# RWKV-7 scan: the prepared product X a taken apart into two products inside each step

## The chip, the cores and the metric

The kernel runs on one core of a Trainium2 chip. The metric is the device time of one execution in microseconds; the median of several executions is quoted. Four engines compute and run side by side, each through its own queue in order: PE (matrix products), DVE (vector), ACT (scalar) and POOL (GpSimd); SP issues the DMAs. They wait for each other by semaphores.

## The reference, cut to what matters

An encoder with four layers. Layers 0 and 3 mix by latent attention, layer 1 by RWKV-7, layer 2 by an RG-LRU; after each mixer stands a convolutional gated feed-forward block. The change touches the recurrence of layer 1 alone: 16 heads of 64, 528 tokens, forwards and backwards.

```python
def _wkv7_scan(r, w, a, b, k, v, reverse):
    def step(S, inp):
        r_t, w_t, a_t, b_t, k_t, v_t = inp
        sa = jnp.einsum('bhvk,bhk->bhv', S, a_t)
        S = S * w_t[:, :, None, :] + sa[..., None] * b_t[:, :, None, :] + v_t[..., None] * k_t[:, :, None, :]
        return S, jnp.einsum('bhvk,bhk->bhv', S, r_t)
    ...
    _, y = lax.scan(step, S0, xs, reverse=reverse)
```

## The kernel before

**The recurrence in windows.** `rwkv_scan` cuts the 528 tokens into nine windows (eight of 64 tokens and one of 16) and works on a pair of heads at a time, one head on partitions 0 to 63 and the other on 64 to 127. Eight pairs and two directions make 16 *chains*, numbered i = 0 to 15. Inside a window the recurrence is solved with a triangular inverse X (tile `xt`); from window to window only the 64x64 state S is handed on.

**What a chain needs.** For each chain four streams of instructions prepare tiles:
- `stage_a`: decays, keys and queries of all windows. `xr[:, 0]` holds the rows a, `xr[:, 1]` the rows r, `bk` the rows b and k; the products of `bk` with `xr`, masked, are `am` (`am[:, 1, w, 0:64]` is A_ak of window w, `am[:, 0, w, 0:64]` is A_ab). `stage_a` also starts the streams below.
- `inverses`: inverts the 16x16 diagonal blocks on POOL, by way of two trips through DRAM (`sc`, `sd`). Its last step on chip is an ACT copy `dt<-dt` that waits for POOL.
- `stage_b`: joins the blocks to the full X in `xt`, with products into the bank `rb` and DVE between them.
- `a_tokens` (turns a into `at`), `bk_tokens` (turns b and k into `tb`), `ak_v` (A_ak v of all windows at once, into `r1`). They use `per_window`: 18 products of 64x64, then two ACT copies out of PSUM, one of 512 columns and one of 64. The end of `stage_b` makes `xa` = X a in the same way.

**A step of a chain** (`chain`, from L1644). For window w the bank `pu` gets X r1, issued one step ahead, and then `xa` times S; DVE copies it to `u`. The bank `ps` gets the products of `tb` with v and with u; DVE turns it into the next state S (tile `s1`), with the decayed old state `sp` from POOL. Products of `am`, `xr` and v, u, S go to `yp`, the output, and are waited for only at the chain's end. So from one S to the next the path runs: PE (`ch<-s,xa`), DVE (`u<-ch`), PE (`ch<-u,tb`), DVE (`s<-ch,pc,sp`). The banks of `pu` and `ps` come from a pool of two, called `ch`. A chain can begin when the chain before it has been issued.

**What sets the order.** `Streams.run` is a list scheduler that runs while the kernel is built. It holds a cost for each operation and a latency for each pair of engines, and writes out one fixed order for each engine; the streams' priorities come from `AHEAD`, and a later chain's preparation is woven between the steps of the chain that runs. Where its plan leaves PE idle for long and the products planned shortly before are few, `fill` puts in products that nobody reads (`idle<-hid_w`, 128x256), called fillers below. On the chip each engine takes its instructions in the written order, whatever the real times are.

One product of 64x64 in the code appears in the trace as two matrix instructions.

Of the kernel before, what the change touches and what calls it, by code (L numbers as in the profile page):

```python
# [143 lines left out]
class Streams:  # L144
# [13 lines left out]
    def take(self, kind):  # L158
        return ("take", kind)

    def give(self, t):
        return ("give", t)

    def wait(self, *names):
        return ("wait", names)

    def spawn(self, name, gen, prio=0.0):
        return ("spawn", name, gen, prio)
# [157 lines left out]
class Kern:  # L326
# [999 lines left out]
    def rwkv_scan(self, es, hid, rkv, yall):  # L1326
        nc, a, tc = self.nc, self.a, self.tc
        sch = Streams(nc, SLACK)
        pe, ve, ac, po, dq = sch.pe, sch.dve, sch.act, sch.pool, sch.dma
# [5 lines left out]
        def tl(shape, name, bufs=1, dt=F32):  # L1335
            return sch.named(cp.tile(shape, dt, name=name, tag=name, bufs=bufs), name, bufs)
# [25 lines left out]
        N9 = NW + 1  # L1362
# [15 lines left out]
        E = [slice(64 * e, 64 * e + 64) for e in range(2)]  # L1378
# [3 lines left out]
        def prio(kind, i):  # L1382
            return AHEAD[kind] - i
# [43 lines left out]
        def turned(src, out):  # L1427

            yield from per_window(lambda w, e: src(w)[E[e]], lambda w, e: self.ident[E[e], E[e]], lambda ps, ws: ac.copy(out[:, ws], ps))
# [40 lines left out]
        def stage_a(i, hp, d, P, U):  # L1470
# [42 lines left out]
            else:  # L1513
                yield ve.scalar_tensor_tensor(out=xr[:, 0, 0:T - 1], in0=kk[:, 0:T - 1], scalar=-2.0, in1=ep[:, 1:T], op0=ALU.mult, op1=ALU.mult)
                yield ve.tensor_scalar(out=xr[:, 0, 63:T:64], in0=kk[:, 63:T:64], scalar1=-2.0, scalar2=None, op0=ALU.mult)
                yield ve.tensor_scalar(out=xr[:, 0, T - 1:T], in0=kk[:, T - 1:T], scalar1=-2.0, scalar2=None, op0=ALU.mult)
            yield spawn(f"at{i}", a_tokens(i, xr, U), prio("at", i))
            yield ve.tensor_tensor(out=xr[:, 1, 0:T], in0=P["r"], in1=ep, op=ALU.mult)
            yield ve.tensor_copy(pc[:, 0:NW], ep[:, (0 if d else 63):SEQ:64])
            yield ve.tensor_copy(pc[:, NW:NW + 1], ep[:, SEQ:SEQ + 1])  # L1520
# [21 lines left out]
                    yield give(pa)  # L1542
            yield spawn(f"inv{i}", inverses(i, d, U), prio("inv", i))
            yield spawn(f"tb{i}", bk_tokens(bk, U), prio("tb", i))
            yield spawn(f"r1{i}", ak_v(i, hp, P, U), prio("r1", i))
            if d:
                yield po.tensor_tensor(out=P["kds"], in0=P["kds"], in1=kd, op=ALU.add)

        def a_tokens(i, xr, U):
            if i >= 2:  # L1550
                yield wait(f"b{i - 2}")
            U["at"] = tl([128, N9, 64], "at", 2)
            yield from turned(lambda w: xr[:, 0, w * 64:w * 64 + 64], U["at"])

        def bk_tokens(bk, U):
            tb = U["tb"] = tl([128, 2, N9, 64], "tb", DEEP)
            for j in range(2):
                yield from turned(lambda w: bk[:, j, w], tb[:, j])

        def ak_v(i, hp, P, U):  # L1560
            yield wait(f"values{hp}", *([f"c{i - 3}"] if i >= 3 else []))
            r1 = U["r1"] = tl([128, N9, 64], "r1", 3)
            yield from per_window(lambda w, e: U["am"][E[e], 1, w, 0:64], lambda w, e: P["vt"][E[e], w], lambda ps, ws: ac.copy(r1[:, ws], ps))

        def inverses(i, d, U):

# [34 lines left out]


        def stage_b(i, hp, d, P, U):
            yield wait(f"inv{i}", f"at{i}", f"r1{i}", *([f"b{i - 1}"] if i else []))
            am, dc = U["am"], U["dc"]
            dd = [tl([128, NW, 4, 16], f"dd{j}") for j in range(2)]
            for j in (1, 0):
                yield ve.tensor_tensor(out=dd[j], in0=dc[:, j].unsqueeze(2).to_broadcast([128, NW, 4, 16]),
                                       in1=blk.unsqueeze(1).to_broadcast([128, NW, 4, 16]), op=ALU.mult)
            dtr, dn = (t.rearrange("p w q t -> p w (q t)") for t in dd)  # L1610
            nn = tl([128, NW, 64], "nn")

            def product(lhsT, rhs):
                ps = yield take("rb")
                for w in range(NW):
                    for e in range(2):
                        r = rhs(w, e)
                        yield pe.matmul(win(ps)[E[e], w, 0:r.shape[-1]], lhsT=lhsT(w, e), rhs=r, start=True, stop=True)
                return ps

            ps = yield from product(lambda w, e: am[E[e], 0, w, 0:64], lambda w, e: dn[E[e], w])
            yield ve.tensor_tensor(out=nn, in0=win(ps), in1=offb.unsqueeze(1).to_broadcast([128, NW, 64]), op=ALU.mult)
            yield give(ps)
            if i >= 2:
                yield wait(f"c{i - 2}")
            xt = U["xt"] = xts[i % 2]
            ps = yield from product(lambda w, e: nn[E[e], w], lambda w, e: dtr[E[e], w])
            yield ve.tensor_tensor(out=xt[:, 0:NW], in0=win(ps), in1=dtr, op=ALU.add)
            yield give(ps)

            b0 = 32 * d
            for lo, hi, c0, c1 in ((b0, b0 + 32, 32 - b0, 64 - b0), (b0, 16 + 48 * d, 48 * (1 - d), 64 - 48 * d)):
                n = c1 - c0
                ps = yield from product(lambda w, e: nn[E[e], w], lambda w, e: xt[E[e], w, c0:c1])
                for e in range(2):
                    r = slice(64 * e + lo, 64 * e + hi)
                    yield ve.tensor_tensor(out=xt[r, 0:NW, c0:c1], in0=win(ps)[r, :, 0:n], in1=dtr[r, :, c0:c1], op=ALU.add)
                yield give(ps)

            xa = U["xa"] = tl([128, N9, 64], "xa", 2)  # L1640
            yield from per_window(lambda w, e: U["at"][E[e], w], lambda w, e: xt[E[e], w], lambda ps, ws: ac.copy(xa[:, ws], ps))


        def chain(i, hp, d, P, U):  # L1644
            yield wait(f"b{i}", f"r1{i}", f"tb{i}", *([f"c{i - 1}"] if i else []))
            am, xr, v, pc, y, tb = U["am"], U["xr"], P["vt"], U["pc"], yall[:, hp], U["tb"]
            u = tl([128, N9, 64], "u")
            yt = yield take("yp")
            yp = win(yt)
            order = list(range(N9))[::-1 if d else 1]  # L1650

            def both(o, lhsT, rhs, start, stop):
                for e in range(2):
                    yield pe.matmul(o[E[e]], lhsT=lhsT[E[e]], rhs=rhs[E[e]], start=start, stop=stop)

            S = None
            pu = yield take("ch")
            yield from both(pu[:, 0:64], U["xt"][:, order[0]], U["r1"][:, order[0]], True, True)
            for w, after in zip(order, order[1:] + [None]):
                n = 16 if w == NW else 64  # L1660
                rw = xr[:, 1, w * 64:w * 64 + n]

                if S is not None:
                    yield from both(pu[:, 0:64], U["xa"][:, w], S, False, True)
                if after is not None:
                    p1 = pc[:, w:w + 1]
                    if S is not None:
                        sp = tl([128, 64], "sp", 2)
                        yield po.tensor_tensor(out=sp, in0=S, in1=p1.to_broadcast([128, 64]), op=ALU.mult)
                    ps = yield take("ch")  # L1670
                    yield from both(ps[:, 0:64], tb[:, 1, w], v[:, w], True, False)
                yield ve.tensor_copy(u[:, w], pu[:, 0:64])
                yield give(pu)
                if after is not None:
                    yield from both(ps[:, 0:64], tb[:, 0, w], u[:, w], False, True)
                    pu = yield take("ch")
                    yield from both(pu[:, 0:64], U["xt"][:, after], U["r1"][:, after], True, False)
                    s1 = tl([128, 64], "s1", 3)
                    if S is None:
                        yield ve.tensor_scalar(out=s1, in0=ps[:, 0:64], scalar1=p1, scalar2=None, op0=ALU.mult)  # L1680
                    else:
                        yield ve.scalar_tensor_tensor(out=s1, in0=ps[:, 0:64], scalar=p1, in1=sp, op0=ALU.mult, op1=ALU.add)
                    yield give(ps)
                yo = (yield take("ps")) if w == NW else yp[:, w]
                yield from both(yo[:, 0:n], v[:, w], am[:, 1, w, 64:64 + n], True, False)
                if S is not None:
                    yield from both(yo[:, 0:n], S, rw, False, False)
                yield from both(yo[:, 0:n], u[:, w], am[:, 0, w, 64:64 + n], False, True)
                if w == NW:
                    if d:  # L1690
                        yield ve.tensor_tensor(out=y[:, SEQ:], in0=y[:, SEQ:], in1=yo[:, 0:16], op=ALU.add)
                    else:
                        yield ac.copy(y[:, SEQ:], yo[:, 0:16])
                    yield give(yo)
                S = s1
            if d:
                yield ve.tensor_tensor(out=w64(y), in0=w64(y), in1=yp, op=ALU.add)
            else:
                yield ac.copy(w64(y), yp)
            yield give(yt)  # L1700
# [204 lines left out]
```

## Time and profile before

| | |
|---|---|
| median of 3 runs | 3550.47 us (3542.97 to 3557.28) |
| profiled execution | 3547.82 us, span 3546.0 us |
| PE busy | 3229.4 us (91% of the span) |
| DVE busy | 2799.9 us (79%) |
| ACT busy | 1610.5 us (45%) |
| POOL busy | 1003.2 us (28%) |
| stage of the 16 chains | from 1099.7 to 1572.8 us |

A busy share is the union of the instructions' durations; products are pipelined and overlap, so a busy PE may still have room. Times inside the span are counted from its start. "Granted clock" is the share of full speed that TensorE's throttle let through.

### The profile page before, as it was taken

To read this page: it belongs to the slowest core of one execution; us is meant where nothing else is said; L and a number is where in the kernel's file an instruction comes from. 1 tells how busy PE (TensorE), PEld (TensorE's weight loads), DVE (VectorE), ACT (ScalarE), POOL (GpSimd) and SP (SyncE) were. 2 spreads that over 40 slices of the span, in tenths; PEclk is the share of its full clock that TensorE was granted. 3 is DMA by queue.
4 is the path that set the end of the run, shared out by engine and by line. 5 is a ranking of instruction groups with operands and counts; after the bars stand their busy time and mean duration, and the time that the engine had idled before them with its cause. 6 is when DMAs were issued, how large, how long until landed. Compare 5 with 4: busy or idle time off the path is not lost.

```text
span 3546.0 us, 77810 instructions
## 1 busy us (share of the span) xinstructions
PE 3229.4 (91%) x31961; PEld 3099.3 (87%) x31961; DVE 2799.9 (79%) x5158; ACT 1610.5 (45%) x3035; POOL 1003.2 (28%) x1438
## 2 busy tenths in 40 slices
PE   5999889997988888878899988989999899989998
PEld 5899889996977877868899988979999799979998
DVE  5877799979436767657999779789997787789997
ACT  4765444333333333324333468643334666543433
POOL 0000253323006455434533200045431000045341
PEclk9999999998989999989999989999999999999999
DMA  2011213322422112122233222213332011212332
GB/s 82 22 40 38 75 63 103 103 84 86 136 77 48 35 38 45 25 53 88 82 105 97 87 72 72 79 54 100 98 94 81 20 37 34 66 43 93 103 92 71
DMA packets 155557, 250.06 MB, mean 71 GB/s; under 512 B 78496, under 2 KB 85824, under 8 KB 154944
## 3 DMA queue, kind: packets, MB, share of 16 engines
q1 hardware_dynamic: 155200, 245.08, 22.7%
q8 instruction: 251, 4.11, 0.5%
q14 instruction: 106, 0.87, 0.1%
HBM read 227.93 MB, written 17.10 MB: 69 GB/s over the span
## 4 chain that ended last, share of the span: by engine, by line
PE 59%; DVE 22%; ACT 8%; issue 5%; POOL 3%; DMA 2%; SPq 0%; DVEq 0%; ACTq 0%; POOLq 0%
PE bank L424 13%; PE bank L422 13%; PE bank L423 13%; PE pj L218 8%; PE ps L218 3%; DVE wlo L577 3%; PE s L218 3%; PE ch L218 1%; ACT wv L218 1%; PE rb L218 1%; DVE cv L699 1%; DVE pst L218 1%; DVE gp L640 1%; DVE cv L705 1%; DVE wlo L411 1%
## 5 line engine op out<-in xcount | busy, mean ns | idle before, releaser
L422 PE MATMUL bank<-xhi,whi 128*128 128x264 f32 x2144 | 608.3, 289 | 38.6 <-ACT xhi L416 28.9
L423 PE MATMUL bank<-xlo,whi 128*128 128x264 f32 x2144 | 618.3, 290 | 23.7 <-DVE xlo L564 12.5
L424 PE MATMUL bank<-xhi,wlo 128*128 128x264 f32 x2144 | 613.0, 289 | 23.4 <-DVE wlo L577 21.6
L422 PEld LDWEIGHTS bank<-xhi,whi 128*128 128x128 f32 x2144 | 406.3, 192 | 41.2 <-ACT xhi L416 28.8
L423 PEld LDWEIGHTS bank<-xlo,whi 128*128 128x128 f32 x2144 | 410.4, 191 | 33.1 <-DVE xlo L564 17.8
L424 PEld LDWEIGHTS bank<-xhi,wlo 128*128 128x128 f32 x2144 | 409.4, 192 | 29.7 <-DVE wlo L577 27.2
L424 PE MATMUL bank<-phi,wlo 128*128 128x264 f32 x1408 | 401.2, 285 | 2.1 <-DVE wlo L411 2.1
L422 PE MATMUL bank<-phi,whi 128*128 128x264 f32 x1408 | 400.5, 284 | 0.0
L423 PE MATMUL bank<-plo,whi 128*128 128x264 f32 x1408 | 400.3, 284 | 0.0
L576 ACT CAST whi<-wraw 128x1024 fp32r<-128x1024 f32 (+1 forms) x240 | 217.3, 907 | 263.9 <-PE bank L423 164.4
L577 DVE TENSOR_TENSOR wlo<-wraw,whi 128x1024 fp32r<-128x1024 f32 (+1 forms) x240 | 321.3, 1340 | 10.5 <-ACT whi L576 10.0
L411 DVE TENSOR_TENSOR wlo<-wraw,whi 128x1024 fp32r<-128x1024 f32 (+1 forms) x218 | 243.7, 1118 | 105.1 <-ACT whi L410 102.3
L410 ACT CAST whi<-wraw 128x1024 fp32r<-128x1024 f32 (+1 forms) x218 | 205.6, 946 | 198.8 <-PE bank L423 140.6
L424 PE MATMUL bank<-thi,wlo 128*128 128x264 f32 x960 | 276.2, 288 | 21.3 <-DVE wlo L577 21.3
L423 PE MATMUL bank<-tlo,whi 128*128 128x264 f32 x960 | 274.7, 286 | 0.0
L422 PE MATMUL bank<-thi,whi 128*128 128x264 f32 x960 | 273.9, 286 | 0.0
L424 PEld LDWEIGHTS bank<-phi,wlo 128*128 128x128 f32 x1408 | 264.8, 188 | 2.8 <-DVE wlo L411 2.8
L422 PEld LDWEIGHTS bank<-phi,whi 128*128 128x128 f32 x1408 | 265.1, 188 | 0.0
L423 PEld LDWEIGHTS bank<-plo,whi 128*128 128x128 f32 x1408 | 264.7, 188 | 0.0
L591 POOL TENSOR_TENSOR wraw<-wraw,wsum 128x512 f32<-128x512 f32 x80 | 113.4, 1418 | 384.7 <-DVE wlo L577 313.1
L424 PEld LDWEIGHTS bank<-thi,wlo 128*128 128x128 f32 x960 | 182.6, 190 | 23.8 <-DVE wlo L577 23.8
L422 PEld LDWEIGHTS bank<-thi,whi 128*128 128x128 f32 x960 | 182.9, 191 | 0.0
(402 smaller groups left out, 9841.1 us busy)
## 6 DMA issues: line engine op xcount, KB each, us to landing
wraw<-in_ffn_in_dram SPq DMA_DIRECT2D x176, 512.0 KB
wraw<-in_ffn_out_dram SPq DMA_DIRECT2D x96, 384.0 KB
wraw<-in_mla_o_dram SPq DMA_DIRECT2D x48, 256.0 KB
wraw<-in_rw_rkv_dram SPq DMA_DIRECT2D x24, 512.0 KB
wraw<-in_lru_in_dram SPq DMA_DIRECT2D x20, 512.0 KB
wraw<-in_mla_q_dram SPq DMA_DIRECT2D x16, 512.0 KB
wraw<-in_ffn_out_dram SPq DMA_DIRECT2D x16, 512.0 KB
rkv<-ro SPq DMA_DIRECT2D x24, 264.0 KB
```

What stands on the lines that cost most here:

```text
L218: op.fn(*op.args, **op.kw)
L410: nc.scalar.copy(hi[:, :cols], raw[:, :cols])
L411: nc.vector.tensor_tensor(out=lo[:, :cols], in0=raw[:, :cols], in1=hi[:, :cols].bitcast(F32), op=ALU.subtract)
L422: nc.tensor.matmul(out, lhsT=w[0][ws], rhs=x[0][xs], start=start, stop=False)
L423: nc.tensor.matmul(out, lhsT=w[0][ws], rhs=x[1][xs], start=False, stop=False)
L424: nc.tensor.matmul(out, lhsT=w[1][ws], rhs=x[0][xs], start=False, stop=stop)
L576: nc.scalar.copy(hi[:, cut], x[:, cut])
L577: nc.vector.tensor_tensor(out=lo[:, cut], in0=x[:, cut], in1=hi[:, cut].bitcast(F32), op=ALU.subtract)
L591: e.tensor_tensor(out=a1[:, 1], in0=a1[:, 1], in1=s[:, 1], op=ALU.subtract)
L640: add = lambda out, x: nc.vector.tensor_tensor(out=out, in0=x, in1=ps, op=ALU.add)
L699: nc.vector.scalar_tensor_tensor(out=c, in0=gp[:, q:q + T], scalar=self.p(f"fc_w{l}{q}", f), in1=c, op0=ALU.mult, op1=ALU.add)
L705: nc.vector.tensor_tensor(out=c, in0=c, in1=dst[j][:, 1:T + 1], op=ALU.mult)
```

## The change

The step computes W = A_ak v + a S first, copies it out of PSUM, and then multiplies by X. The stream `a_tokens` with its tile `at`, the stream `ak_v` with `r1`, and the product `xa` at the end of `stage_b` are gone; `stage_b` and `chain` no longer wait for them, and `chain` waits for `values` (the tile `vt` of v) instead. A step takes three banks one after the other from the same pool of two: `pw`, `ps`, `pu`.

```diff
@@ stage_a
-            yield spawn(f"at{i}", a_tokens(i, xr, U), prio("at", i))
...
-            yield spawn(f"r1{i}", ak_v(i, hp, P, U), prio("r1", i))
...
-        def a_tokens(i, xr, U):
-            if i >= 2:
-                yield wait(f"b{i - 2}")
-            U["at"] = tl([128, N9, 64], "at", 2)
-            yield from turned(lambda w: xr[:, 0, w * 64:w * 64 + 64], U["at"])
...
-        def ak_v(i, hp, P, U):
-            yield wait(f"values{hp}", *([f"c{i - 3}"] if i >= 3 else []))
-            r1 = U["r1"] = tl([128, N9, 64], "r1", 3)
-            yield from per_window(lambda w, e: U["am"][E[e], 1, w, 0:64], lambda w, e: P["vt"][E[e], w], lambda ps, ws: ac.copy(r1[:, ws], ps))
@@ stage_b
-            yield wait(f"inv{i}", f"at{i}", f"r1{i}", *([f"b{i - 1}"] if i else []))
+            yield wait(f"inv{i}", *([f"b{i - 1}"] if i else []))
...
-            xa = U["xa"] = tl([128, N9, 64], "xa", 2)
-            yield from per_window(lambda w, e: U["at"][E[e], w], lambda w, e: xt[E[e], w], lambda ps, ws: ac.copy(xa[:, ws], ps))
@@ chain
-            yield wait(f"b{i}", f"r1{i}", f"tb{i}", *([f"c{i - 1}"] if i else []))
+            yield wait(f"b{i}", f"values{hp}", f"tb{i}", *([f"c{i - 1}"] if i else []))
...
-            pu = yield take("ch")
-            yield from both(pu[:, 0:64], U["xt"][:, order[0]], U["r1"][:, order[0]], True, True)
+            pw = yield take("ch")
+            yield from both(pw[:, 0:64], am[:, 1, order[0], 0:64], v[:, order[0]], True, True)
...
-                    yield from both(pu[:, 0:64], U["xa"][:, w], S, False, True)
+                    yield from both(pw[:, 0:64], xr[:, 0, w * 64:w * 64 + 64], S, False, True)
+                x = tl([128, 64], "x", 2)
+                yield ac.copy(x, pw[:, 0:64])
+                yield give(pw)
...
+                pu = yield take("ch")
+                yield from both(pu[:, 0:64], U["xt"][:, w], x, True, True)
                 yield ve.tensor_copy(u[:, w], pu[:, 0:64])
                 yield give(pu)
...
-                    pu = yield take("ch")
-                    yield from both(pu[:, 0:64], U["xt"][:, after], U["r1"][:, after], True, False)
+                    pw = yield take("ch")
+                    yield from both(pw[:, 0:64], am[:, 1, after, 0:64], v[:, after], True, False)
```

Since the scheduler writes the order anew, rows move on every engine. On PE, in the last chain, two steps before the change stand like this (`ch<-s,xa` is X a times S, `ch<-r,xt` is X r1 of the next step, `ch<-u,tb` the product that makes the next state; "x2" is the two heads):

```order
L218 MATMUL ch_20280<-s_20283,xa 64x64 x2
L218 MATMUL ch_20295<-vt_11278,tb 64x64 x2
L218 MATMUL ch_20295<-u,tb 64x64 x2
L218 MATMUL ch_20301<-r_19508,xt_11280 64x64 x2
L218 MATMUL yp_20184<-am,vt_11278 64x64 x2
L218 MATMUL yp_20184<-xr,s_20283 64x64 x2
L218 MATMUL yp_20184<-am,u 64x64 x2
L218 MATMUL ch_20301<-s_20304,xa 64x64 x2
```

and after the change, at the same place (`ch<-s,xr` is a S, `ch<-x,xt` is X W, `ch<-vt,am` is A_ak v of the next step):

```order
L218 MATMUL ch_19993<-s_19996,xr 64x64 x2
L218 MATMUL ch_20010<-vt_11278,tb 64x64 x2
L218 MATMUL ch_20013<-x,xt_11280 64x64 x2
L1739 MATMUL idle<-hid_w_9613 128x256 x4
L218 MATMUL ch_20010<-u,tb 64x64 x2
L218 MATMUL ch_20023<-vt_11278,am 64x64 x2
L218 MATMUL yp_19861<-am,vt_11278 64x64 x2
L218 MATMUL yp_19861<-xr,s_19996 64x64 x2
L218 MATMUL yp_19861<-am,u 64x64 x2
L218 MATMUL ch_20023<-s_20026,xr 64x64 x2
```

A third product on the path, `ch<-x,xt`, now stands between the product with S and the one with u, and in this step four fillers behind it.

In the middle of the stage, where later chains are prepared, a step before the change has on PE (`rb` is `stage_b` of a later chain, `ps<-ident,bk` its `bk_tokens`):

```order
L218 MATMUL ch_16266<-s_16269,xa 64x64 x2
L218 MATMUL ch_16285<-vt_11278,tb 64x64 x2
L218 MATMUL rb_16230<-dd_16177,am 64x64 x7
L218 MATMUL ch_16285<-u,tb 64x64 x2
L218 MATMUL ch_16298<-r_15073,xt_11280 64x64 x2
L218 MATMUL ps_16146<-vt_11277,am 64x64 x9
```

and after it, at a similar place:

```order
L218 MATMUL ch_16586<-s_16591,xr 64x64 x2
L218 MATMUL rb_16520<-dd_16384,nn 64x64 x4
L218 MATMUL ch_16613<-vt_11277,tb 64x64 x2
L218 MATMUL rb_16520<-dd_16384,nn 64x64
L218 MATMUL ch_16616<-x,xt_11279 64x64 x2
L218 MATMUL ps_16563<-hid_a_9653,w2hi 128x264
L218 MATMUL ps_16563<-hid_a_9653,w2lo 128x264
L218 MATMUL ps_16555<-rs_y,rwcst 128x132
...
L218 MATMUL ch_16613<-u,tb 64x64 x2
```

The preparation is now dealt out over three gaps of a step in place of two; the nine `ps<-vt,am` (the batched A_ak v) have no counterpart.

On ACT, behind the copy `dt<-dt` that waits for POOL, stands before the change, at two places in the middle of the stage:

```order
L218 COPY dt<-dt 66x256
L218 COPY at<-ps_15442 128x512
L218 COPY at<-ps_15479 128x64
...
L218 COPY dt<-dt 66x256
L218 ACTIVATE c<-ps_16060,half_b 128x264
L218 COPY tb<-ps_16144 128x512
```

and after it, at two places there:

```order
L218 COPY dt<-dt 66x256
L218 COPY x<-ch_15213 128x64
L218 ACTIVATE c<-ps_15267,half_b 128x264
L218 COPY x<-ch_15259 128x64
...
L218 COPY dt<-dt 66x256
L218 COPY x<-ch_15766 128x64
L218 COPY x<-ch_15818 128x64
```

The copy `x` of the running chain stands directly behind `dt<-dt` at ten of its sixteen places; before, no instruction of a running step was on ACT.

## Rows read from the trace of the kernel before

**Rows 1.** The page: the span, and each engine's busy time.
```profile
span 3546.0 us, 77810 instructions
PE 3229.4 (91%) x31961; PEld 3099.3 (87%) x31961; DVE 2799.9 (79%) x5158; ACT 1610.5 (45%) x3035; POOL 1003.2 (28%) x1438
```
**Rows 2.** Windows: ahead of the chains, the stage of the chains, behind it.
```profile
core 0: us, PE busy (x) PEld busy (x) DVE busy (x) ACT busy (x) POOL busy (x), PEclk, DMA share, GB/s
1070.00:1100.00 30.00, 22.98 (x479) 19.52 (x478) 16.80 (x39) 11.76 (x28) 22.62 (x59) 0.89 0.30 65
1099.70:1572.80 473.10, 417.98 (x9542) 379.70 (x9540) 308.90 (x840) 142.84 (x341) 239.12 (x600) 0.95 0.17 35
1580.00:1600.00 20.00, 13.30 (x74) 12.48 (x73) 10.23 (x17) 8.94 (x15) 2.17 (x3) 0.62 0.55 187
```
**Rows 3.** Tile u: duration ns min/median/max, first and last start us.
```profile
L218 PE MATMUL ch<-u,tb x512: 216/218/367, 1101.8 to 1571.4; 64*64 64x64 f32 x171
L218 DVE COPY u<-ch x144: 199/224/226, 1100.7 to 1572.4; 128x64 f32<-128x64 f32 x144
```
**Rows 4.** Timeline, one step of the last chain: start us, duration us.
```profile
1563.02 0.28 DVE L218 SCALAR_TENSOR_TENSOR s<-ch,pc,sp 128x64 f32<-128x64 f32 x1 [0.51 <-PE ch L218]
...
1563.36 0.33 PE L218 MATMUL ch<-s,xa 64*64 64x64 f32 x4
...
1563.74 0.22 DVE L218 COPY u<-ch 128x64 f32<-128x64 f32 x1 [0.43 <-PE ch L218]
1564.02 0.33 PE L218 MATMUL ch<-u,tb 64*64 64x64 f32 x4 [0.21 <-DVE u L218]
...
1564.47 0.28 DVE L218 SCALAR_TENSOR_TENSOR s<-ch,pc,sp 128x64 f32<-128x64 f32 x1 [0.50 <-PE ch L218]
...
1564.81 0.33 PE L218 MATMUL ch<-s,xa 64*64 64x64 f32 x4
```
**Rows 5.** Timeline of PE: runs of equal products, with the row behind.
```profile
1355.32 0.37 PE L218 MATMUL ps<-hid_a,w2hi 128*128 128x264 f32 x1
1355.53 0.28 PE L218 MATMUL ps<-hid_a,w2lo 128*128 128x264 f32 x1
1355.74 1.09 PE L218 MATMUL ps<-xr,bk 64*64 64x128 f32 x16
1356.66 0.28 PE L218 MATMUL yp<-am,vt 64*64 64x64 f32 x4
...
1360.08 1.15 PE L218 MATMUL ps<-ident,bk 64*64 64x64 f32 x32
1361.06 0.28 PE L218 MATMUL ch<-u,tb 64*64 64x64 f32 x4
...
1019.98 2.18 PE L1751 MATMUL idle<-hid_w 128*128 128x256 f32 x17
```
**Rows 6.** Timeline: an ACT copy of 64 columns behind its products.
```profile
1305.09 0.35 PE L218 MATMUL ps<-ident,bk 64*64 64x64 f32 x4
...
1305.48 0.21 ACT L218 COPY tb<-ps 128x64 f32<-128x64 f32 x1 [0.46 <-PE ps L218]
```
**Rows 7.** Groups by form, 1100 to 1573 us: busy, mean ns, idle before.
```profile
L218 PE MATMUL ps<-vt,am 64*64 64x64 f32 x468 | 28.4, 221 | 0.0
L218 PE MATMUL ps<-xt,at 64*64 64x64 f32 x541 | 27.3, 239 | 5.6 <-DVE xt L218 4.2 <-ACT xa L218 0.7 <-DVE kkh L218 0.5
L218 PE MATMUL ps<-ident,xr 64*64 64x64 f32 x504 | 21.3, 234 | 3.8 <-DVE xr L218 3.7
```
**Rows 8.** Waits, 1100 to 1573 us: total us, times, longest us.
```profile
ACT dt L218 <- POOL dt L218: 33.0, 12, 6.7
PE ch L218 <- DVE u L218: 11.6, 23, 2.7
PE ch L218 <- DVE s L218: 7.5, 12, 1.6
```

## The prediction

> **What bounds the kernel now.** The page comes first: PE is busy for 91% of the span [rows 1], but that is an average over stages, and the change touches one. The tile `u` shows which: its first copy starts at 1100.7 us and its last at 1572.4 us [rows 3]. The windows give this stage: 473.1 us, PE busy for 418 of it at a granted clock of 0.95, DVE for 309, POOL for 239, ACT for 143 [rows 2]. PE is the fullest engine, yet its durations overlap, so I ask how much of the stage PE's queue fills when it never waits.
>
> For that I count PE's rows in the written order from the first `ch<-u,tb` of the first chain to the last of the last, and price them by runs without a wait [rows 5]. The run of 32 instructions of 64x64 (16 rows of the order) starts at 1360.08 and the next begins at 1361.06: 0.0615 us a row. Eight rows of 64x128 take 0.92 us: 0.115 each. A row of 128x264 takes 0.21 us; a filler (2.18 - 0.28) / 16 = 0.119 us. The order has 3471 rows of 64x64, 468 of 64x128, 166 of 128x264, 10 fillers and some 690 others, mostly of 32 or 16 columns at about the small price. The queue's sum is **363.6 us**. The stretch itself, from the first to the last start of `ch<-u,tb`, is 1571.4 - 1101.8 = **469.6 us** [rows 3]. So 106 us are not PE's own work.
>
> The other limit is the chain's path. The last chain has nothing beside it and shows its bare hops [rows 4]: from `ch<-s,xa` (1563.36) by the copy `u` to `ch<-u,tb` (1564.02) 0.66 us, from there by `s` to the next `ch<-s,xa` (1564.81) 0.79 us, a step of 1.45 us. Over 144 steps that is 209 us, under half the stage: most hops hide behind rows of later chains. A hop costs PE something only where the rows written between its two ends last less than the hop. In the order before I find 74 of 255 hops too short in this sense, by **10.8 us** in all. What is left, 469.6 - 363.6 - 10.8 = **95.2 us**, I call the rest: waits for the preparation and for busy engines, real durations over the planner's, and stretches at the lower clock. The waits of PE for `u` and `s` alone (11.6 and 7.5 us [rows 8]) show that hops are a small part of it.
>
> **The change part by part.** *Removed:* in that stretch of the order 451 rows of 64x64 are gone on balance (3471 to 3020): the turn of a, the batched A_ak v, X a and X r1, less the new A_ak v and X W. 451 x 0.0615 = 27.7 us. The whole kernel loses 576 such rows, 35.4 us; the other 125 stand mostly ahead of the first step, where PE has gaps already (23.0 of 30 us busy [rows 2]), and I take them as worth nothing; if they were on the path it would be 7.7 us. Four rows of 128x132 also move out (0.9 us). On ACT the copies of `at`, `r1` and `xa` go (two per tile and chain, 96 in all), on an engine busy 30% of the stage.
>
> *Added to the queue:* the planner puts 129 fillers where there were 10: 119 x 0.119 = 14.2 us. They stand in gaps that the plan has; where the real gap is as long they cost nothing, else their own time. I count them as queue, and shortages behind them. The queue becomes **349.0 us**, 14.6 less.
>
> *Added to the path:* one hop a step, by ACT. The trace has no `x` copy, so I bound it: an ACT copy of 64 columns takes 0.21 us and starts 0.04 us after the modelled end of its products [rows 6], the DVE copy of `u` 0.22 us and 0.05 us [rows 4]. So a hop by ACT is one by DVE: 0.66 us, 0.79 at most by the other hop. Bare, a step is 1.45 + 0.66 = 2.11 us. At the two ends: nothing where other rows fill it, and 144 x 0.66 = 95 us where none do. Where it falls is read from the order again. Of 384 hops in the stretch, 190 are too short: 63 from X W to u, 85 from u to S, 42 from S to X W; 21.0 + 9.5 + 14.1 = **44.6 us**. The cause stands in the order quoted: the same preparation is dealt over three gaps instead of two, and fewer rows are there to deal. In the last chain, with no cover, eight steps at 0.66 are 5.3 us of it.
>
> *Moved:* no DMA. The waits for `at` and `r1` fall; PE idled 5.6 us ahead of `ps<-xt,at` and 3.8 us ahead of `ps<-ident,xr`, and nothing ahead of `ps<-vt,am` [rows 7]. But most of the first is a wait for `xt`, which X W now waits for in the same place. Against these 9.4 us stands a new exposure: behind a late ACT copy the whole step is queued, PE's next rows with it. I let the two cancel and keep the rest at 95.2 us. If the 9.4 us did go, the sum would be that much lower; if the rest grew with the number of hops (399 groups of products on the path against 256), it would be 148 us, 53 more.
>
> *Sum:* 349.0 + 44.6 + 95.2 = 488.8 us against 469.6: **19 us longer**. The profiled execution's 3547.8 us become 3567; it lies 2.7 us under the median of the runs, 3550.5, so on that scale **3570 us**, 0.5% slower.
>
> **The rivals.** A change of 0.5% (18 us) is about what a measurement of this kernel can tell from none.
>
> *PE's work alone decides (faster).* If PE stands for the rest anyway, the short hops fall into those waits, and only the queue counts: -14.6 us, and -24 us if the waits ahead of the removed products go too: 3526 to 3536 us. For it speaks that the rest is 95 us and PE the fullest engine; against it that 95 us over 255 hops is too thin to swallow 34 more in every place, and that the last chain has no rest at all. It decides from the point where over half of the added 34 us is absorbed.
>
> *Half absorbed (no change).* 14.6 us less queue, 17 us more shortage: 3553 us.
>
> *ACT's queue holds the chain.* `x` stands directly behind `dt<-dt` at ten of sixteen places, and ACT waited 33.0 us, up to 6.7 at a time, in 12 such copies for POOL [rows 8]. Before, that held nothing urgent. At 33.0 / 12 = 2.75 us each, ten are 27 us on top of my sum: 3597 us. Against it: part of that wait was ACT having nothing earlier to do. The Trainium skill (TensorE: Matmul & The Clock Gate, "Architectural detail") states that ACT and DVE take instructions strictly in order; no row here shows ACT overtaking, so by that rule the block is real whenever POOL is late.
>
> *The clock falls.* The granted clock is 0.95 in the stage, and 0.62 from 1580 us, where PE is busy for 13.3 of 20 us [rows 2]; 0.95 already means stretches at 1.2 in place of 2.4 GHz. More standing could bring more of them: at 0.90 the 349 us of rows would take 349 x (0.95/0.90 - 1) = 19 us more, 3589 us. The fillers are there against it. The Trainium skill (the same page, "Loop structure matters more than you think") says that bursts of matmuls with waits between them go cold; the window behind the stage agrees, and by that rule a change that adds waits pays a second time.
>
> **How the numbers follow.** My forecast has a chance of 0.45, with its own range from 3555 to 3585 us; PE's work alone 0.2; half absorbed 0.1; ACT's queue 0.15; the clock 0.1. The predicted time is the forecast's, 3570 us. The range leaves out half of the first rival below and the upper part of the last two with the growth of the rest above: 3530 to 3610 us. By 0.5% of the median the bounds are 3533 and 3568. Faster is most of the first rival, 0.18; slower is over half of the forecast (0.26) and the last two rivals, 0.51; the same is what is left, 0.31.
>
> **What would show it.** The stage from the first to the last `ch<-u,tb` should last about 489 us; the last chain's step 2.1 us against 1.45; the copy `x` about 0.21 us, some 0.04 us behind its product. PE's waits ahead of `ch<-x,xt` and `ch<-u,tb` should be the largest of the stage, and larger than the 19 us for `u` and `s` before. Outside the stage nothing should move. I am wrong if the stage gets shorter (the rest swallowed the hops), if ACT's `x` starts late behind `dt<-dt` by microseconds, or if the granted clock of the stage leaves 0.95 by more than 0.02.

## The result, and the profile after

The changed kernel takes 3580.39 us (median of 5 runs, 3573.92 to 3585.35) against 3550.47; the ratio is **1.0084 (95% interval 1.0067 to 1.0102)**. The forecast was 3570 us and slower; the time is 10 us above it, inside the range. The profile after is of the fastest of these five executions (3573.92 us), so a stretch of another run set against it can look some 6 us longer than the medians say.

The page's head of the changed kernel answers to [rows 1]:

```profile
span 3572.1 us, 75878 instructions
...
PE 3253.9 (91%) x30934; PEld 3107.2 (87%) x30934; DVE 2803.7 (78%) x5158; ACT 1604.8 (45%) x3083; POOL 994.6 (28%) x1438
```

PE has 1027 instructions fewer and yet is busy 24.5 us longer. The span grew by 26.1 us. The tiles `u` and `ch` of the changed kernel (duration min/median/max in ns, first and last start in us) say where it grew, beside [rows 3]:

```profile
L218 PE MATMUL ch<-u,tb x512: 215/219/368, 1104.1 to 1596.7; 64*64 64x64 f32 x171
L218 ACT COPY x<-ch x144: 189/212/233, 1102.1 to 1597.8; 128x64 f32<-128x64 f32 x144
```

The stretch that the prediction summed, from the first to the last start of `ch<-u,tb`, is 1596.7 - 1104.1 = **492.6 us**, against 469.6 before and 489 forecast: 23.0 us longer, where 19 were forecast. It also starts 2.3 us later. The copy `x` takes 0.212 us, as the nearest row had said.

One step of the last chain in the changed kernel (timeline, start and duration in us), beside [rows 4]:

```profile
1588.24 0.33 PE L218 MATMUL ch<-s,xr 64*64 64x64 f32 x4
...
1588.68 0.21 ACT L218 COPY x<-ch 128x64 f32<-128x64 f32 x1 [2.20 <-PE ch L218]
1588.94 0.33 PE L218 MATMUL ch<-x,xt 64*64 64x64 f32 x4 [0.25 <-ACT x L218]
1589.32 0.23 DVE L218 COPY u<-ch 128x64 f32<-128x64 f32 x1 [1.13 <-PE ch L218]
1589.60 0.33 PE L218 MATMUL ch<-u,tb 64*64 64x64 f32 x4 [0.33 <-DVE u L218]
...
1590.05 0.28 DVE L218 SCALAR_TENSOR_TENSOR s<-ch,pc,sp 128x64 f32<-128x64 f32 x1 [0.50 <-PE ch L218]
...
1590.39 0.33 PE L218 MATMUL ch<-s,xr 64*64 64x64 f32 x4
```

The bare hop by ACT is 1588.94 - 1588.24 = 0.70 us, the hop by DVE again 0.66, and the step 2.15 us against 1.45. PE stands idle in front of two of the three products of the path: 0.25 us for `x` and 0.33 us for `u`.

The waits in the stage of the changed kernel (total us, times, longest us), beside [rows 8]:

```profile
PE ch L218 <- DVE u L218: 26.4, 37, 2.8
PE ch L218 <- ACT x L218: 9.2, 29, 0.8
ACT dt L218 <- POOL dt L218: 8.1, 8, 1.7
PE ch L218 <- DVE s L218: 4.5, 13, 1.0
```

PE's waits for the running step's copies went from 19.1 to 40.1 us, most of it for `u`. ACT's wait for POOL went from 33.0 to 8.1 us. And the stretch's window, columns as in [rows 2]:

```profile
1104.10:1596.70 492.60, 435.93 (x8658) 380.58 (x8659) 306.62 (x831) 139.03 (x396) 230.57 (x595) 0.92 0.16 34
```

The granted clock is 0.92 where it was 0.95. Of the three signs by which the prediction said it would be wrong, this one came.

A second reading shows what the sum hid. The copies `u<-ch` mark the chains, nine to a chain. The windows of chain 7 before, from its first such copy to its last and from there to the first of chain 8 (columns as in [rows 2]):

```profile
1315.21:1339.20 23.99, 20.54 (x488) 18.45 (x484) 13.75 (x35) 7.07 (x17) 15.03 (x40) 1.00 0.17 28
1339.20:1354.22 15.02, 12.28 (x224) 10.94 (x220) 13.48 (x32) 6.93 (x17) 9.16 (x20) 0.89 0.27 77
```

and the same two in the changed kernel:

```profile
1337.77:1365.27 27.50, 24.91 (x554) 22.63 (x554) 19.01 (x48) 8.88 (x24) 16.75 (x39) 1.00 0.28 68
1365.27:1371.64 6.37, 3.00 (x42) 1.98 (x36) 5.90 (x13) 2.90 (x10) 4.74 (x10) 1.00 0.03 7
```

Inside the chain 24.0 us became 27.5; between the chains 15.0 us became 6.4. Summed over all chains in this way, the time inside them went from 347 to 447 us, the time between them from 124 to 48 us. So a step grew by 100 / 128 = 0.78 us. That is not all hop. PE did not stand between the chains before: it was busy for 104 of the 124 us, with 1976 matrix instructions, among them 508 of X a and 447 of `stage_b` (`rb<-xt,nn`). In the changed kernel 368 are left there; X a is gone and `rb<-xt,nn` stands wholly inside the chains, which hold 8323 instructions where they held 7542. At the prediction's prices of a row, 54 us of the 100 are rows that now lie inside the chains, and 70 of the 77 us that came back are rows that no longer lie between them.

### The profile page after: what moved, and what is told of

It reads as the page before. It is cut to its first block, busy times and chain, and to the rows that moved or that the text cites. A ratio compares the mean times of both kernels' runs of the same rounds, so it can differ in the third digit from the quotient of the medians.

```text
span 3572.1 us, 75878 instructions
## 1 busy us (share of the span) xinstructions
PE 3253.9 (91%) x30934; PEld 3107.2 (87%) x30934; DVE 2803.7 (78%) x5158; ACT 1604.8 (45%) x3083; POOL 994.6 (28%) x1438
## 4 chain that ended last, share of the span: by engine, by line
PE 43%; DVE 16%; ACT 5%; issue 4%; POOL 1%; DMA 1%; SPq 0%; DVEq 0%; ACTq 0%; POOLq 0%
PE bank L424 9%; PE bank L423 9%; PE bank L422 9%; PE pj L218 4%; PE ps L218 3%; PE ch L218 3%; DVE wlo L577 2%; PE rb L218 1%; PE s L218 1%; PE yp L218 1%; DVE cv L699 1%; DVE gp L640 1%; PE mm L423 1%; PE mm L424 1%; DVE cv L705 1%
```

## The experiments

Four ideas are to be told apart. *The path*: queue of PE's rows, plus short hops, plus a rest. *PE's work alone*: only the queue counts. *The clock*: the granted clock falls. *ACT's queue* holding `x`. "Stretch" is always first to last start of `ch<-u,tb`, from each run's own trace; ratios are to the kernel before.

**The hop alone** (e1_hop_alone), on the kernel before:

```diff
+                x = tl([128, 64], "x", 2)
+                yield ac.copy(x, pu[:, 0:64])
+                yield give(pu)
+                pu = yield take("ch")
+                for e in range(2):
+                    yield pe.matmul(pu[E[e], 0:64], lhsT=self.ident[E[e], E[e]], rhs=x[E[e]], start=True, stop=True)
                 yield ve.tensor_copy(u[:, w], pu[:, 0:64])
```

> The kernel before with one useless hop in each step: the bank pu is copied by ACT to x, multiplied by the identity, and only then copied to u; nothing is taken away. Theory of the path (queue of PE's rows, plus hops that have too few rows between their ends, plus a rest of 95 us): the written order gives a queue of 385.8 us and 145 short hops with 34.5 us, so 516 us from the first to the last ch<-u,tb against 470, 46 us more than before (3597 us). Theory that PE's work alone decides: only the queue's 22 us more (3573 us). Theory that the bare hop is on the path at every step: 95 us more (3645 us).

Measured: 3595.58 us, ratio 1.0116 (1.0097 to 1.0136), 41 us more; the stretch is 508.4 us, 39 more. PE's work alone (22 us) and the full bare hop (95 us) both miss; the path's 46 is nearest. Inside the chains it is 92 us more (439), between them 52 less (72), and here too it is mostly the order: at the same prices 75 us of rows more lie inside and 53 us fewer between.

**The work alone** (e2_work_alone), on the kernel before:

```diff
-            yield spawn(f"at{i}", a_tokens(i, xr, U), prio("at", i))
...
-            yield spawn(f"r1{i}", ak_v(i, hp, P, U), prio("r1", i))
...
-            xa = U["xa"] = tl([128, N9, 64], "xa", 2)
-            yield from per_window(lambda w, e: U["at"][E[e], w], lambda w, e: xt[E[e], w], lambda ps, ws: ac.copy(xa[:, ws], ps))
...
-                    yield from both(pu[:, 0:64], U["xa"][:, w], S, False, True)
+                    yield from both(pu[:, 0:64], zero[:, w], S, False, True)
...
-                    yield from both(pu[:, 0:64], U["xt"][:, after], U["r1"][:, after], True, False)
+                    yield from both(pu[:, 0:64], U["xt"][:, after], zero[:, after], True, False)
```

> The kernel before with the streams for at, r1 and xa left out and a tile of zeros in the place of r1 and xa, so that a step has the products, hops and waits of before (it leaves out the a and A_ak v terms of the recurrence, the output is not the reference's). Theory of the path: queue 325.2 us, short hops 13.4 us, rest 95 us: 434 us against 470, 36 us less (3515 us). If PE's work is covered by waits anyway: no change (3550 us). If the clock falls as the queue thins: the granted clock in the stage under 0.92 and less than half of the 36 us.

Measured: 3541.32 us, ratio 0.9972 (0.9960 to 0.9984), 11 us less; the stretch is 460.0 us, 10 less where the path said 36. A miss, and a telling one. Its window, ACT's wait for POOL, and PE's longest wait of the preparation:

```profile
1100.10:1560.10 460.00, 399.46 (x8036) 357.92 (x8037) 303.64 (x831) 112.78 (x255) 237.98 (x595) 0.89 0.17 35
```

```profile
ACT dt L218 <- POOL dt L218: 94.9, 13, 14.1
PE rb L218 <- DVE xt L218: 16.0, 15, 3.7
```

Rows of 38 us left PE's queue, nearly all of them from between the chains, but the time between the chains is still 104 us and inside them 358. Between the chains PE now stands idle for 29 us where it stood for 21. ACT waits 94.9 us for POOL's inverses, but that is not PE's wait; what holds PE most in the preparation is DVE's `xt`, 16.0 us against 6.5 before. That the length of the preparation takes over as soon as PE is lighter is likely, and not shown. The clock fell too, to 0.89, which is what the third case had said; the two explanations are not parted by this run. Either way the work that the change removes is worth about 10 us without the hop, not its price on PE.

**The copy on DVE** (e3_x_on_dve), on the changed kernel:

```diff
-                yield ac.copy(x, pw[:, 0:64])
+                yield ve.tensor_copy(x, pw[:, 0:64])
```

> The changed kernel with the copy x on DVE in place of ACT. If ACT's queue holds the chain, this takes the hold away: up to 27 us less than the changed kernel (3553 us). Theory of the path: a hop by DVE is as long, DVE is the fuller engine (308 of 497 us against 140), and the written order has 54.0 us of short hops against 44.6: 0 to 10 us more than the changed kernel (3580 to 3590 us).

Measured: 3611.86 us, ratio 1.0171 (1.0154 to 1.0189), 31 us over the changed kernel, stretch 534.8 us. Taking `x` off ACT gained nothing. By itself this does not clear ACT's queue, since it cost three times what the path by rows had allowed: PE waits 23.8 us for `x` and 20.5 for `u`, both now in the fuller engine's queue, and the clock is 0.85. The changed kernel's own trace settles it: from the modelled end of its products to its start, `x` takes 0.10 us in the median of 144 copies and over 1 us in three (1.2 at most); what goes beyond 0.10 us adds up to 12 us, for `u` on DVE to 37. PE's waits with `x` on DVE:

```profile
PE ch L218 <- DVE x L218: 23.8, 40, 1.8
PE ch L218 <- DVE u L218: 20.5, 46, 1.9
```

**No fillers** (e4_no_fill), the changed kernel with `NEED = 0` in place of 4300:

> The changed kernel without any filler. Theory of the path: queue 333.8 us and short hops 58.1 us in place of 349.1 and 44.6: 2 us less than the changed kernel (3578 us), if the clock stays. Theory of the clock: the granted clock in the stage falls clearly under 0.92 (to 0.8 or less) and the time grows by 349 x (0.92/0.80 - 1) = 50 us or more (3630 us).

Measured: 3587.04 us, ratio 1.0099 (1.0084 to 1.0114), 7 us over the changed kernel, with intervals that overlap; stretch 509.5 us, 17 more, at a clock of 0.83:

```profile
1099.20:1608.70 509.50, 438.72 (x8528) 387.28 (x8530) 307.12 (x831) 139.07 (x396) 234.29 (x598) 0.83 0.16 33
```

The queue is 15 us shorter and the stretch longer. The path had put the stretch 2 us under the changed kernel's, so some 19 us are left over. The clock can carry them, by rows of the kernel before: a run of 32 instructions of 64x64 that took 0.98 us at a granted clock of 1.00 [rows 5] stands there at 0.50 too, and takes 1.71 us, 0.023 us more for each instruction:

```profile
1261.14:1262.85 1.71, 1.71 (x38) 1.71 (x36) 1.47 (x3) 0.00 (x0) 1.63 (x3) 0.50 0.36 84
```

In the stretch 509 matrix instructions start at the lower level in the kernel before, 742 in the changed one, 1646 here. An estimate from these: 904 x 0.023 = 21 us here against the changed kernel, if all of them are on the path. Dividing the queue by the clock, 334 x (1/0.83 - 1/0.92) = 39 us, would be twice what is left over.

**More fillers** (`NEED = 5500`), on the three kernels:

> The kernel with the work left out (zeros in the place of r1 and xa, as in the run of the work alone; its output is not the reference's), and with more fillers (NEED 5500 in place of 4300; 140 in the stretch against 77, so the queue is 332.7 us against 325.2, short hops 10.6 against 13.4). Theory of path and clock: the granted clock of the stretch was 0.89 in the run of the work alone and 0.95 before; with the clock back at 0.95 the stretch takes 332.7/0.95 + 10.6 + 80 = 441 us against 460, 19 us less in spite of the longer queue (3522 us). Theory of the path without the clock: 5 us more (3546 us).

> The kernel before with NEED 5500: 48 fillers in the stretch against 10, queue 368.2 us against 363.6, short hops 8.9 against 10.8. Theory of path and clock: at a clock of 0.98 in place of 0.95, 368.2/0.98 + 8.9 + 76 = 461 us against 470, 9 us less (3542 us). Without the clock: 3 us more (3555 us).

> The changed kernel with NEED 5500: 283 fillers in the stretch against 129, queue 367.4 us against 349.1, short hops 39.1 against 44.6. Theory of path and clock: at a clock of 0.97 in place of 0.92, 367.4/0.97 + 39.1 + 69 = 487 us against 493, 6 us less than the changed kernel (3574 us), so that the hop remains the greater part of the loss. If the clock were all of the loss: back to the time before (3552 us). Without the clock: 13 us more (3593 us).

Measured: the work alone 3548.17 us, ratio 0.9975 (0.9966 to 0.9984), stretch 464.4, 4 us more than with fewer fillers; before 3557.65 us, ratio 1.0012 (1.0002 to 1.0022), stretch 474.1, 4.5 more; changed 3597.95 us, ratio 1.0119 (1.0102 to 1.0136), stretch 511.3, 19 more. The added fillers price at 7.5, 4.6 and 18 us of queue. The forecasts with the clock all fell, those without it held within 5 us: the clock hardly rose (0.89 to 0.91, 0.95 to 0.95, 0.92 to 0.93), and in the two whole kernels the fillers cost about their own time. The window of the changed kernel with them:

```profile
1104.40:1615.70 511.30, 458.65 (x8812) 399.81 (x8813) 305.25 (x831) 140.28 (x396) 229.20 (x595) 0.93 0.16 32
```

**The last two chains as before** (e8_last_two_old), on the changed kernel:

```diff
-                sch.add(f"c{i}", chain(i, hp, d, P, U), prio("c", i))
+                sch.add(f"c{i}", (chain_old if i >= OLD else chain)(i, hp, d, P, U), prio("c", i))
```

Here `OLD` is 14, and the streams for `at` and `r1` and the product `xa` run for chains 14 and 15 alone.

> The changed kernel with the last two chains (14 and 15) in the form of before; their a, A_ak v and X a are prepared again. Nothing is left to lie beside the hops there. Theory of the path: the last chain's step goes from 2.15 back to 1.45 us, 8 x 0.7 = 5.6 us less in that chain and part of as much in the one before; 5 to 10 us less than the changed kernel (3570 to 3575 us). If the loss sits in the middle of the stage (clock, ACT's or DVE's queue): no change beyond the noise.

Measured: 3579.07 us, ratio 1.0068 (1.0053 to 1.0084), no change beyond the noise against the changed kernel: the medians are 1 us apart, the ratios 6 us, too close to tell the path's 5 to 10 us from none. In the last chain the step did go back to 1.45 us:

```profile
1589.78 0.23 DVE L219 COPY u<-ch 128x64 f32<-128x64 f32 x1 [0.96 <-PE ch L219]
1591.23 0.23 DVE L219 COPY u<-ch 128x64 f32<-128x64 f32 x1 [0.25 <-PE ch L219]
```

The two chains took 14.3 and 11.6 us in place of 21.2 and 18.3, 13.6 less, and the stretch is 4.8 us longer all the same (497.4). The other chains and the times between them grew by 18 us, at a clock of 0.88. Why the middle of the stage got slower is not settled. The clock is the one difference that shows in the window: 1118 instructions start at the lower level where 742 did, some 9 us by the estimate above. And a new order of rows comes with every edit.

**The hop twice** (e9_hop_twice): the lines added in the hop alone, put into the changed kernel ahead of the copy to `u`.

> The changed kernel with a second useless hop in each step (pu copied by ACT to x2, times the identity, then to u). The first hop alone cost the kernel before 39 us of stretch. If each hop has the same price: 39 us more than the changed kernel (3620 us). Theory of the path: the cover is used up by the first hop; in the changed kernel the time between chains is down to 48 us from 124, so nearly the whole bare hop shows, 144 x 0.70 = 101 us more; the written order says a queue of 391.8 us and 338 short hops with 102 us, 589 us in all or 96 us more (3677 us).

Measured: 3689.26 us, ratio 1.0380 (1.0358 to 1.0402), 109 us over the changed kernel; stretch 617.2 us, 125 more, in an execution 8 us over the median. One more hop costs about three times the first one. Not all of it is hop: by the forecast's order 43 us are queue, 25 of them 212 fillers more, and 57 us are short hops, 100 in all where the trace has 125. The stretch is read from the tile `u`:

```profile
L218 PE MATMUL ch<-u,tb x512: 216/246/366, 1104.2 to 1721.4; 64*64 64x64 f32 x171
```

**sp on ACT** (e10_before_sp_act, e11_after_sp_act), on the kernel before and on the changed one:

```diff
-                        yield po.tensor_tensor(out=sp, in0=S, in1=p1.to_broadcast([128, 64]), op=ALU.mult)
+                        yield ac.activation(out=sp, in_=S, func=AF.Identity, scale=p1)
```

> The kernel before with the decayed old state sp made by ACT (activation with a scale per partition) in place of POOL. POOL waited 168 us for S in front of sp, with the inverses of later chains queued behind. If that holds up the preparation and so the 124 us between the chains: ACT's waits for POOL (33 us) go and the stretch loses 20 us or more (3530 us). Theory of the path by rows alone: queue 365.7 us, short hops 12.2 us, 3 us more (3556 us).

> The changed kernel with sp on ACT. The time between its chains is 48 us and ACT waits only 8 us for POOL, so the preparation no longer holds the chains: no gain. Theory of the path by rows: queue 349.7 us, short hops 49.9 us, 6 us more than the changed kernel (3587 us); if ACT's queue is the hold, with 112 more instructions on it: 15 us more or worse (3597 us).

Measured: before 3560.59 us, ratio 1.0021 (1.0009 to 1.0034), 6 us more; changed 3596.97 us, ratio 1.0126 (1.0108 to 1.0143), 17 us over the changed kernel. Freeing POOL gained nothing; ACT still waited 24.1 us for POOL in the first. In the second PE waits 14.5 us for `x` where it waited 9.2, and 33.1 for `u` where it waited 26.4, at a clock of 0.89. So a fuller ACT may hold the chain a little; this run does not part that from the rest.

No run here beats the kernel before and keeps its computation.

## Why the prediction was right, point by point

**The sum.** It gave 349.0 + 44.6 + 95.2 = 489 us for the stretch; the trace has 492.6. With queue and short hops as counted, the rest is 99.0. Under four microseconds off, and 2.3 more because the first step comes later, which the sum had at nothing. Between the medians it is 30 us where the profiled executions give 26 (3573.9 against 3547.8); the remaining few lie within the spread of the runs.

**The hop.** "A hop by ACT is one by DVE: 0.66 us, 0.79 at most": 0.70 us measured, inside the bounds; the 0.04 us more are a later start, 0.10 us behind the modelled end of its products where 0.04 had been read. The short hops from X W to u, from u to S and from S to X W had been put at 21.0, 9.5 and 14.1 us; PE waited 26.4 us for `u`, 4.5 for `s` and 9.2 for `x`. The wait for `u` is PE's largest, as forecast; the one for `x` is third, behind 10.6 us for `xt` in `stage_b`. In the kernel before the same count gave 10.8 us where PE waited 19.1, so the count is no exact price. Put in by itself, the hop cost 39 us of stretch where 46 were forecast.

**The step that was mis-sized: the removed work.** The prediction counted "451 x 0.0615 = 27.7 us" as a gain at full price. In the run of the work alone 38 us of queue gave 10. About 10 us of what was lost can be the clock (959 instructions at the lower level against 509, by the same estimate); how the others come about stays open.

**Luck in the size.** The runs lead from the kernel before to the changed one by two ways, and the hop alone and the changed kernel have equally many products in a step. Hop first: forecast +46 and then -27 for the removed work, measured +39 and -16. Work first: forecast -36 and then +55 for the hop, measured -10 and +33. (By the medians it is +41 and -15, -11 and +39.) Both ways the hop and the removed work were priced too high, and in the difference, 19 us forecast and 23 measured, most of that cancels. That the hop costs more than the removed work gives back is shown on both ways; that the sum came within 4 us is in part luck. It shows in the term that was kept: the rest, put at 95.2 us for any order, came out from 88 us (the hop alone) to 123 (the hop twice) in the eleven traces whose queue and short hops were counted. In the six of them with up to 751 instructions at the lower clock it was 88 to 105 us, in the five with 892 or more 115 to 123: the rest goes with the clock, though no run sets the clock by itself.

**What covers the hop.** The prediction had rows of PE between the hop's ends as its cover, and the traces bear that out: the planner put 54 us of rows more into the chains' steps, 10 of them fillers, most of the others from between the chains. PE's idle time in the stretch (its length less PE's busy time) hardly moved with the first hop: 55.0 us before, 51.0 with the hop alone, 56.7 after. Between the chains of the changed kernel some 22 us of rows are left, at the prediction's prices, of the 92 before, so the second hop found few to draw in: with it PE's idle time is 77.5 us, and its waits for `x` are 31.1 us where they were 9.2. That this is why it cost more than the first is likely, and not shown, since the planner also added fillers.

**The rivals.** *PE's work alone* is out by the sign, and by the hop alone (39 us for 22 of queue). *ACT's queue* is out for this change: the wait for POOL fell to 8.1 us, and `x` started over 1 us late in three of 144 places. *Half absorbed*, no change, is out: the interval starts at 1.0067. *The clock* came in part: 0.92, which the prediction had said would make it wrong. Dividing the queue, 349 x (1/0.92 - 1/0.95) = 12 us would be its share; by the instructions at the lower level, (742 - 509) x 0.023, it is about 5 us, an estimate. More fillers did not bring the clock back, so its share could not be taken away and measured. The Trainium skill (TensorE: Matmul & The Clock Gate, "Loop structure matters more than you think") says that PE goes cold where a long wait for DMA stands between matmuls. The waits that the change adds are for copies, 2.8 us at the longest, so no run here tests that; the direction agrees, with 0.95 before, 0.92 after and 0.83 without fillers.

**Fillers.** They were counted as queue. Added ones did cost about their own time (18 us of queue, 19 of stretch), yet taking all away cost 17 of stretch, 7 by the medians: of the three settings tried the planner's was the fastest.

## What to carry to other kernels

Before adding a hop to a serial chain, ask what work can lie between its ends and where that work lies now: here the first hop drew rows in from between the chains and cost 39 us of its bare 95, and a second one found few left and cost 125, fillers included. Work taken from the busiest engine need not be worth its time: leave that work out without the hop and see. Where all engines run written orders, counting an engine's rows between the two ends of each hop gave the sign of the change and its total within 4 us in 490, but the same count missed by 26 us for the work alone and 28 for the hop twice. So the parts must be tested one at a time, best by two ways to the same kernel.

## What was not expected

The granted clock of this stage ran from 0.95 down to 0.83 over small edits of the order, and did not follow the number of fillers: 129 gave 0.92, 283 gave 0.93, none gave 0.83. An ACT copy of 64 columns out of PSUM made a bare hop of 0.70 us, 0.04 longer than the DVE copy, though the instruction itself is the shorter one (0.212 against 0.224 us): in the last chain it starts 0.10 us behind the modelled end of its products, the DVE copy 0.05.
